# First token tile's index and DSA scores as two reduced-precision passes over the whole array, in place of float32 products on 64-row halves

## The chip, the cores and the metric

One NeuronCore of one Trainium2 chip runs the whole kernel. The metric is device microseconds of one execution. TensorE (PE in the views) does the matrix products, VectorE (DVE) and ScalarE (ACT) everything that is done by element, GpSimd (POOL) next to nothing, and SyncE (SP) issues nearly all the loads.

## The reference, cut to what matters

A decoder trunk of two layers on 256 tokens of width 1024, in float32. Each layer mixes tokens in two ways from one projection `h @ w_in`, gates and adds the two, and then runs a SwiGLU feed-forward part. The second mixer, DSA, is the one that the change touches. It scores every earlier token with a light indexer, keeps the 64 best for each query, and attends to those alone:

```python
rel = relu(einsum('bthd,bsd->bths', iq_i, ik))        # 8 index heads, 64 wide, one shared index key
score = einsum('bths,bth->bts', rel, iw_i)
score = where(key_pos <= t, score, -inf)
_, sel = lax.top_k(score, k_top)                      # 64 of the earlier tokens
s = einsum('bthd,btkhd->bhtk', q_i, gather(k, sel)) * ATTN_SCALE   # 8 heads, 64 wide
p = _masked_softmax(s, valid)
out = einsum('bhtk,btkhd->bthd', p, gather(v, sel))
```

Both score products contract over 64 numbers, half of the 128 rows of TensorE's array.

## The kernel before

The 256 tokens are two tiles of 128 (`i = 0` and `i = 1`). Weights come from memory in pieces of 1024 columns a partition (`raw`). ScalarE rounds a piece to `hi` (L164) and VectorE takes the rest as `lo` (L165). Both have the type float32r, a float32 that TensorE takes in one pass. Each dense product is three such passes (`mul3`, L173 to L175), and these 3,282 products are most of what TensorE does. The first token tile's queries see only the first 128 keys, so its score blocks are 128 x 128; the second tile's are 128 x 256.

A score product with 64 wide heads is written in one of two ways.

For the second token tile, `stack` or `twice` writes a head's rounded part and its rest into the two 64-row halves of one 128-row block, and the other operand twice, so that two float32r passes over the whole array (`score`, L335) give the product. Stacked index queries lie in `iqs`, rounded and remaining index keys in `iks`, stacked DSA keys in `dks`, doubled DSA queries in `dqs`. `iqs` and `dks` share their memory with the NSA queries `qs` (tag "qs"), `dqs` and `iks` share theirs with the NSA keys (tag "ks").

For the first token tile, plain float32 operands (`iqT`, `ikT`, `dqT`, `dkT`) are multiplied on 64 rows: even heads on rows 0 to 63, odd heads on rows 64 to 127 (L433 for the index, L661 for DSA). In the trace a float32 product shows as two records and a float32r product as one, so the 8 calls of L433 or L661 in a layer are 16 records.

Other float32 products on part of the array matter for the order: the values products of NSA and DSA (`values`, L607 and L649) use 64 of the 128 columns, and the hidden layer of NSA's compression (L517, weights `w` loaded by L515) uses 32 of them.

A scheduler decides the order of the instructions on each engine from the dependences and from its own model of time; only a few stretches are fixed by hand. Dense products of the next projection lie between the scores, the softmax steps and the values products.

Of the kernel before, what the change touches and what calls it, by code (L numbers as in the profile page):

```python
# [9 lines left out]
F32 = mybir.dt.float32  # L10
F32R = mybir.dt.float32r
AF = mybir.ActivationFunctionType
# [4 lines left out]
P = 128  # L17
SEQ = 256
NT = SEQ // P
# [12 lines left out]
HALF = (slice(0, 64), slice(64, 128))  # L32
# [47 lines left out]
def hybrid_trunk(ctx: ExitStack, tc: tile.TileContext, a: dict, out: bass.AP):  # L80
    nc = tc.nc
# [5 lines left out]
    one = ctx.enter_context(tc.tile_pool(name="one", bufs=1))  # L87
    work = ctx.enter_context(tc.tile_pool(name="work", bufs=2))
# [9 lines left out]
    def yv_bank():  # L98
        return bank("yv", 1)

    def tr_bank():
        return bank("tr", 2)

    def sc_bank():
        return bank("sc", 2)
# [209 lines left out]
    def stack(dst, src):  # L315

        for e in range(2):
            nc.scalar.activation(dst[e][HALF[e]], src[HALF[e]], AF.Copy)
        for e in range(2):
            nc.vector.tensor_sub(dst[e][HALF[1 - e]], src[HALF[e]], dst[e][HALF[e]].bitcast(F32))  # L320

    def twice(dh, dl, src):

        for e in range(2):
            nc.scalar.activation(dh[e][HALF[e]], src[HALF[e]], AF.Copy)
            nc.any.tensor_copy(dh[e][HALF[1 - e]], src[HALF[e]])
        for e in range(2):
            for h in (e, 1 - e):
                nc.vector.tensor_sub(dl[e][HALF[h]], src[HALF[e]], dh[e][HALF[e]].bitcast(F32))

    def score(o, q, k):

        pairs = [(q, t) for t in k] if isinstance(k, (list, tuple)) else [(t, k) for t in q]
        for n, (u, v) in enumerate(pairs):
            nc.tensor.matmul(o, u, v, start=n == 0, stop=n == 1)  # L335
# [3 lines left out]
    def causal(i):  # L339
        return ALL[:, P:2 * P] if i == 0 else ALL  # L340
# [12 lines left out]
    for l in range(DEPTH):  # L353
# [4 lines left out]
        ga = one.tile([P, KF * SEQ], F32, tag="bigA", name="ga")  # L358
        gb = one.tile([P, KF * SEQ], F32, tag="bigB", name="gb")

        def carve(t, o, *shape):
            n = int(np.prod(shape))
            v = t[:, o:o + n]
            return v.rearrange("p (a b) -> p a b", a=shape[0]) if len(shape) == 2 else v
# [3 lines left out]
        qT, dqT = carve(ga, 2608, 4, SEQ), carve(ga, 3632, 4, SEQ)  # L368
        accs = carve(ga, 4656, NT, SEQ)

        ks = one.tile([P, 4, NT, 2 * P], F32R, tag="ks", name="ks")
        kh, kl = [ks[:, g] for g in range(2)], [ks[:, 2 + g] for g in range(2)]
        qs = one.tile([P, 2, 4, SEQ], F32R, tag="qs", name="qs")
        ikT = carve(ga, 5168, P)
        gates = carve(gb, 0, NT, 2 * D)
        pji = carve(gb, 4096, NT, 648)
        dkT = carve(gb, 4096, 4, SEQ)
# [19 lines left out]
            load_rest(pji[:, 0, 0:1])  # L397
        iw = small.tile([P, NT, 8], F32, tag="iw", name="iw", bufs=1)
        dbias = []
        iqs = one.tile([P, 2, 4, SEQ], F32R, tag="qs", name="iqs")[:, :, :, 0:P]  # L400
        iks = one.tile([P, 4, NT, 2 * P], F32R, tag="ks", name="iks").rearrange("p a b t -> p a (b t)")[:, 0:2, 0:SEQ]
        for i in range(NT):
            nc.vector.tensor_scalar_mul(iw[:, i], pji[:, i, 576:584], 512 ** -0.5)
            rope(pji[:, i, 0:576].rearrange("p (h d) -> p h d", d=64), i, (9,))
            nc.vector.tensor_copy(pji[:, i, 576:640], pji[:, i, 512:576])
            tok = slice(i * P, (i + 1) * P)
            qp = tr_bank()
            for k in range(4):
                nc.tensor.transpose(qp[:, k * P:(k + 1) * P], pji[:, i, k * P:(k + 1) * P], ident)
            q3 = qp.rearrange("p (k t) -> p k t", t=P)  # L410
            if i == 0:
                iqT = work.tile([P, 4, P], F32, tag="pr", name="iqT", bufs=8)
                nc.scalar.activation(iqT, q3, AF.Copy)
            else:
                stack([iqs[:, e] for e in range(2)], q3)
            kp = tr_bank()[:, 0:P]
            nc.tensor.transpose(kp, pji[:, i, 512:640], ident)
            nc.scalar.activation(iks[:, 0, tok], kp, AF.Copy)
            if i == 0:
                nc.scalar.activation(ikT, kp, AF.Copy)  # L420
            nc.vector.tensor_sub(iks[:, 1, tok], kp, iks[:, 0, tok].bitcast(F32))
        for i in range(NT):
            nk = P * (i + 1)
            acc = accs[:, i, 0:nk]
            prev = causal(i)
            per = 512 // nk
            for p0 in range(0, 4, per):
                sbs = [sc_bank() for _ in range(2)]
                for p in range(p0, p0 + per):
                    outs = [sb[:, (p - p0) * nk:(p - p0 + 1) * nk] for sb in sbs]  # L430
                    if i == 0:
                        for e in range(2):
                            nc.tensor.matmul(outs[e], iqT[HALF[e], p], ikT[HALF[e]], start=True, stop=True)  # L433
                    else:
                        for e in range(2):
                            score(outs[e], iqs[:, e, p], [iks[:, z] for z in range(2)])
                for e in range(2):
                    rl = work.tile([P, 512], F32, tag="k2", name="rl", bufs=3)
                    nc.scalar.activation(rl, sbs[e], AF.Relu)
                    for p in range(p0, p0 + per):  # L440
                        h = 2 * p + e
                        nc.vector.scalar_tensor_tensor(acc, rl[:, (p - p0) * nk:(p - p0 + 1) * nk],
                                                       iw[:, i, h:h + 1], prev, ALU.mult, ALU.add)
                        prev = acc
            dbias.append(acc)
# [23 lines left out]
        for i in range(NT):  # L469
# [12 lines left out]
            kp = tr_bank()  # L482
# [3 lines left out]
            tok = slice(i * P, (i + 1) * P)  # L486
# [3 lines left out]
            q3 = qp.rearrange("p (r t) -> p r t", t=P)  # L490
# [7 lines left out]
        for kind, nm in ((0, "cmpk"), (1, "cmpv")):  # L498
# [9 lines left out]
            for half in range(2):  # L508
                q = 32 * (2 * half + kind)
                for mq in range(2):  # L510
                    r0 = half * 1024 + mq * 512
                    w1 = work.tile([P, 4, P], F32, tag="w1", name="w1", bufs=3)
# [3 lines left out]
                    for m in range(4):  # L516
                        nc.tensor.matmul(hp[q:q + 32, 0:P], blk[:, half * 8 + mq * 4 + m], w1[:, m],  # L517
                                         start=mq == 0 and m == 0, stop=mq == 1 and m == 3, tile_position=(0, q))
# [5 lines left out]
        t = small.tile([P, 2, 2, 16], F32, tag="gt", name="gt", bufs=1)  # L524
# [10 lines left out]
        kp = sc_bank()  # L535
# [102 lines left out]
        def dsa(i):  # L638
            tok = slice(i * P, (i + 1) * P)
            nk = P * (i + 1)  # L640
            per = 512 // nk
            yd = yv_bank()

            def values(p0, pts):
                for p in range(p0, p0 + per):
                    for b in range(i + 1):
                        for e in range(2):
                            v0 = (2 * p + e) * 64
                            nc.tensor.matmul(yd[e * 64:(e + 1) * 64, p * P:(p + 1) * P], dv[:, b, v0:v0 + 64],  # L649
                                             pts[e][:, (p - p0) * (i + 1) + b], start=p == 0 and b == 0,  # L650
                                             stop=p == 3 and b == i)

            done = []
            for p0 in range(0, 4, per):
                pts = []
                sbs = [sc_bank() for _ in range(2)]
                for p in range(p0, p0 + per):
                    outs = [sb[:, (p - p0) * nk:(p - p0 + 1) * nk] for sb in sbs]
                    if i == 0:
                        for e in range(2):  # L660
                            nc.tensor.matmul(outs[e], dqT[HALF[e], p, 0:P], dkT[HALF[e], p, 0:P], start=True, stop=True)  # L661
                    else:
                        for e in range(2):
                            score(outs[e], [dqs[:, z, p] for z in (e, 2 + e)], dks[:, e, p])
                for sb in sbs:
                    segs = sb.rearrange("p (h b t) -> p h b t", h=per, t=P)
                    pts.append(softmax([segs[:, h] for h in range(per)], dbias[i], None))
                done.append((p0, pts))
                if len(done) > LAG:
                    values(*done.pop(0))  # L670
            for d in done:
                values(*d)
            y_out(yd, 4, tok)
# [2 lines left out]
            nsa(i)  # L676

        dks = one.tile([P, 2, 4, SEQ], F32R, tag="qs", name="dks")
        dqs = one.tile([P, 4, NT, 2 * P], F32R, tag="ks", name="dqs").rearrange("p z b (c t) -> p z (b c) t", t=P)
        stack([dks[:, e] for e in range(2)], dkT)  # L680
        twice([dqs[:, e] for e in range(2)], [dqs[:, 2 + e] for e in range(2)], dqT[:, :, P:])
        dsa(0)
        dsa(1)


# [93 lines left out]
        for c0 in range(0, D_FF, 512):  # L779
# [12 lines left out]
            for i in range(NT):  # L792
# [3 lines left out]
                nk = n // P  # L796
# [3 lines left out]
                ks = slice(c0 // P, c0 // P + nk)  # L800
# [72 lines left out]
```

## Time and profile before

| | |
|---|---|
| median of 3 runs | 821.17 us (820.97 to 821.17) |
| the profiled execution | 821.0 us |
| its span, first to last instruction | 819.2 us |
| mean granted TensorE clock | 0.999 of full speed |
| TensorE, matrix products | 810.9 us busy, 4437 records |
| VectorE | 549.5 us busy |
| ScalarE | 461.3 us busy |
| read from memory | 138.24 MB, 170 GB/s over the span |

1.8 us of the profiled execution lie around the span. The time of one record in a list is its whole way through the array, and the next record starts long before it ends; what a record costs TensorE is the distance between starts.

### The profile page before, as it was taken

To read this page: it belongs to the slowest core of one execution; us is meant where nothing else is said; L and a number is where in the kernel's file an instruction comes from. 1 tells how busy PE (TensorE), PEld (TensorE's weight loads), DVE (VectorE), ACT (ScalarE), POOL (GpSimd) and SP (SyncE) were. 2 spreads that over 40 slices of the span, in tenths; PEclk is the share of its full clock that TensorE was granted. 3 is DMA by queue.
4 is the path that set the end of the run, shared out by engine and by line. 5 is a ranking of instruction groups with operands and counts; after the bars stand their busy time and mean duration, and the time that the engine had idled before them with its cause. 6 is when DMAs were issued, how large, how long until landed. Compare 5 with 4: busy or idle time off the path is not lost.

```text
span 819.2 us, 12201 instructions
## 1 busy us (share of the span) xinstructions
PE 810.9 (99%) x4437; PEld 679.2 (83%) x4437; DVE 549.5 (67%) x1201; ACT 461.3 (56%) x791; POOL 8.4 (1%) x18
## 2 busy tenths in 40 slices
PE   8999999999999999999999999999999999999997
PEld 7887888888888888988898888888888888889886
DVE  5799668887665555554577994889776556546445
ACT  6866358773655445444467644778556445444433
POOL 0100000000000000000000000000000000000000
PEclk9999999999999999999999999999999999999999
DMA  8955754125475664576376564542345665547651
GB/s 275 343 165 168 218 172 138 52 81 180 152 231 164 196 183 152 169 241 193 102 214 191 170 207 142 153 129 78 128 134 175 206 192 183 182 119 231 202 177 52
DMA packets 76332, 140.09 MB, mean 171 GB/s; under 512 B 5056, under 2 KB 24512, under 8 KB 76272
## 3 DMA queue, kind: packets, MB, share of 16 engines
q1 hardware_dynamic: 76032, 138.59, 54.2%
q0 software_dynamic: 240, 0.72, 0.4%
q8 instruction: 35, 0.57, 0.3%
q14 instruction: 25, 0.20, 0.1%
HBM read 138.24 MB, written 1.05 MB: 170 GB/s over the span
## 4 chain that ended last, share of the span: by engine, by line
PE 98%; DMA 1%; SPq 0%; ACT 0%; DVE 0%; issue 0%; POOLq 0%; ACTq 0%
PE mm L175 26%; PE mm L173 26%; PE mm L174 26%; PE tr L280 3%; PE sc L335 2%; PE sc L517 2%; PE yv L607 2%; PE yv L175 2%; PE yv L174 2%; PE yv L173 1%; PE tr L798 1%; PE yv L649 1%; DMA raw<-w_in 1%; PE tr L234 1%; PE yv L634 1%; PE sc L174 0%
## 5 line engine op out<-in xcount | busy, mean ns | idle before, releaser
L165 DVE TENSOR_TENSOR lo<-raw,hi 128x1024 fp32r<-128x1024 f32 (+3 forms) x264 | 301.7, 1148 | 159.2 <-ACT hi L164 155.4
L164 ACT ACTIVATE hi<-raw 128x1024 fp32r<-128x1024 f32 (+3 forms) x264 | 262.2, 1000 | 189.3 <-PE mm L175 129.0
L174 PE MATMUL mm<-lo,ah 128*128 128x512 f32 (+3 forms) x850 | 318.9, 375 | 0.0
L175 PE MATMUL mm<-hi,al 128*128 128x512 f32 (+3 forms) x850 | 318.6, 376 | 0.0
L173 PE MATMUL mm<-hi,ah 128*128 128x512 f32 (+3 forms) x850 | 317.5, 379 | 0.0
L175 PEld LDWEIGHTS mm<-hi,al 128*128 128x128 f32 x850 | 159.8, 188 | 28.4 <-issue 1.5
L174 PEld LDWEIGHTS mm<-lo,ah 128*128 128x128 f32 x850 | 160.1, 188 | 26.8 <-issue 0.3
L173 PEld LDWEIGHTS mm<-hi,ah 128*128 128x128 f32 x850 | 159.7, 188 | 27.1 <-ACT hi L164 0.3
L300 ACT ACTIVATE pr<-pr,mx 128x128 f32<-128x128 f32 (+1 forms) x96 | 42.7, 448 | 12.4 <-DVE mx L297 12.1
L174 PE MATMUL mm<-lo,hh 128*128 128x512 f32 x126 | 49.3, 391 | 0.0
L175 PE MATMUL mm<-hi,hl 128*128 128x512 f32 x126 | 49.1, 390 | 0.0
L173 PE MATMUL mm<-hi,hh 128*128 128x512 f32 x126 | 48.7, 395 | 0.0
L803 DVE TENSOR_TENSOR hl<-tr,hh 128x512 fp32r<-128x512 f32 (+1 forms) x24 | 15.5, 647 | 36.5 <-ACT hh L802 36.5
L802 ACT ACTIVATE hh<-tr 128x512 fp32r<-128x512 f32 (+1 forms) x24 | 13.5, 562 | 45.4 <-PE tr L798 45.4
L175 PEld LDWEIGHTS mm<-hi,hl 128*128 128x128 f32 x126 | 23.7, 188 | 4.9
L174 PEld LDWEIGHTS mm<-lo,hh 128*128 128x128 f32 x126 | 23.7, 188 | 4.1
L173 PEld LDWEIGHTS mm<-hi,hh 128*128 128x128 f32 x126 | 23.7, 188 | 4.2
L309 DVE TENSOR_SCALAR pr<-pr,c 128x128 f32<-128x128 f32 (+1 forms) x96 | 24.7, 316 | 0.6
L297 DVE CUSTOM_DVE_ANT_0 pr<-sc,cst 128x128 f32<-128x128 f32 (+1 forms) x64 | 19.0, 353 | 6.3 <-PE sc L335 6.0
L280 PE MATMUL tr<-cst,pr 128*128 128x128 f32 x144 | 20.7, 273 | 0.0
L789 ACT ACTIVATE sg<-mm,rstd 128x512 f32<-128x512 f32 (+1 forms) x24 | 15.7, 654 | 8.8 <-PE mm L175 8.6
L281 ACT COPY pt<-tr 128x512 f32<-128x512 f32 x32 | 17.6, 584 | 4.4 <-PE tr L280 4.4
(247 smaller groups left out, 800.3 us busy)
## 6 DMA issues: line engine op xcount, KB each, us to landing
raw<-w_in SPq DMA_DIRECT2D x72, 512.0 KB, 3.7
raw<-w_ffn_down SPq DMA_DIRECT2D x44, 512.0 KB, 4.4
raw<-w_ffn_gate SPq DMA_DIRECT2D x40, 512.0 KB, 4.5
raw<-w_ffn_up SPq DMA_DIRECT2D x40, 512.0 KB, 4.3
raw<-w_out SPq DMA_DIRECT2D x16, 512.0 KB, 4.1
raw<-w_in SPq DMA_DIRECT2D x16, 292.0 KB, 3.7
raw<-w_branch_nsa SPq DMA_DIRECT2D x16, 256.0 KB, 3.9
raw<-w_branch_dsa SPq DMA_DIRECT2D x8, 512.0 KB, 3.7
```

What stands on the lines that cost most here:

```text
L164: nc.scalar.activation(hi[:, 0:kt * n], raw[:, 0:kt * n], AF.Copy)
L165: nc.vector.tensor_sub(lo[:, 0:kt * n], raw[:, 0:kt * n], hi[:, 0:kt * n].bitcast(F32))
L173: nc.tensor.matmul(dst, xh, wh, start=first, stop=False)
L174: nc.tensor.matmul(dst, xh, wl, start=False, stop=False)
L175: nc.tensor.matmul(dst, xl, wh, start=False, stop=last)
L280: nc.tensor.transpose(tp[:, k * P:(k + 1) * P], piece, ident)
L281: nc.any.tensor_copy(dst, tp[:, 0:len(parts) * P].rearrange("p (k t) -> p k t", t=P))
L297: nc.vector.tensor_tensor_reduce(pr[:, h].rearrange("p (b t) -> p b t", t=P), v, b3, -0.125, 3.4e38, ALU.add, ALU.min, accum_out=mx[:, h:h ...
L300: nc.scalar.activation(pr[:, h], pr[:, h], AF.Exp, bias=mx[:, h:h + 1], scale=-1.0, accum_out=sm[:, h:h + 1])
L309: nc.vector.tensor_scalar_mul(pr[:, h], pr[:, h], c[:, h:h + 1])
L335: nc.tensor.matmul(o, u, v, start=n == 0, stop=n == 1)
L517: nc.tensor.matmul(hp[q:q + 32, 0:P], blk[:, half * 8 + mq * 4 + m], w1[:, m], start=mq == 0 and m == 0, stop=mq == 1 and m == 3, tile_pos ...
```

## The change

For the first token tile too, both scores are now two float32r passes over the whole array. The index queries of both tiles are stacked in `iqs`, and the copies `iqT` and `ikT` go. For DSA, the queries of the first tile are doubled and split into four new tiles `dq0` (three in the memory of tag "q2", one in that of tag "w1", which the compression weights use), and the keys come from the stacked `dks`, which the second tile used already. In a layer, 8 float32 calls for the index and 8 for DSA become 16 float32r calls each.

```diff
@@ -371,7 +371,6 @@
-        ikT = carve(ga, 5168, P)
@@ -397,7 +396,7 @@
-        iqs = one.tile([P, 2, 4, SEQ], F32R, tag="qs", name="iqs")[:, :, :, 0:P]
+        iqs = one.tile([P, 2, 4, SEQ], F32R, tag="qs", name="iqs")
@@ -408,16 +407,10 @@
-            if i == 0:
-                iqT = work.tile([P, 4, P], F32, tag="pr", name="iqT", bufs=8)
-                nc.scalar.activation(iqT, q3, AF.Copy)
-            else:
-                stack([iqs[:, e] for e in range(2)], q3)
+            stack([iqs[:, e, :, tok] for e in range(2)], q3)
             kp = tr_bank()[:, 0:P]
             nc.tensor.transpose(kp, pji[:, i, 512:640], ident)
             nc.scalar.activation(iks[:, 0, tok], kp, AF.Copy)
-            if i == 0:
-                nc.scalar.activation(ikT, kp, AF.Copy)
@@ -428,12 +421,8 @@
-                    if i == 0:
-                        for e in range(2):
-                            nc.tensor.matmul(outs[e], iqT[HALF[e], p], ikT[HALF[e]], start=True, stop=True)
-                    else:
-                        for e in range(2):
-                            score(outs[e], iqs[:, e, p], [iks[:, z] for z in range(2)])
+                    for e in range(2):
+                        score(outs[e], iqs[:, e, p, i * P:(i + 1) * P], [iks[:, z, 0:nk] for z in range(2)])
@@ -656,12 +645,8 @@
-                    if i == 0:
-                        for e in range(2):
-                            nc.tensor.matmul(outs[e], dqT[HALF[e], p, 0:P], dkT[HALF[e], p, 0:P], start=True, stop=True)
-                    else:
-                        for e in range(2):
-                            score(outs[e], [dqs[:, z, p] for z in (e, 2 + e)], dks[:, e, p])
+                    for e in range(2):
+                        score(outs[e], [dqs[i][z][:, p] for z in (e, 2 + e)], dks[:, e, p, 0:nk])
@@ -676,9 +661,12 @@
-        dqs = one.tile([P, 4, NT, 2 * P], F32R, tag="ks", name="dqs").rearrange("p z b (c t) -> p z (b c) t", t=P)
+        dq1 = one.tile([P, 4, NT, 2 * P], F32R, tag="ks", name="dqs").rearrange("p z b (c t) -> p z (b c) t", t=P)
+        dqs = [[work.tile([P, 4, P], F32R, tag=t, name="dq0", bufs=3) for t in ("q2", "q2", "q2", "w1")],
+               [dq1[:, z] for z in range(4)]]
+        twice(dqs[0][0:2], dqs[0][2:4], dqT[:, :, 0:P])
         stack([dks[:, e] for e in range(2)], dkT)
-        twice([dqs[:, e] for e in range(2)], [dqs[:, 2 + e] for e in range(2)], dqT[:, :, P:])
+        twice(dqs[1][0:2], dqs[1][2:4], dqT[:, :, P:])
```

The scheduler also puts other work in other places. Three of them, all on TensorE, follow; `sc`, `tr`, `yv` and `mm` are the accumulator banks of scores, transposes, values and dense products, and a row with `x7` stands for seven calls. Line numbers behind the change are up to 12 lower.

The first is the index in layer 0. Before, its rows are these (dense products are left out):

```order
L409 MATMUL tr<-cst,gb 128x128 x4
L433 MATMUL sc<-ga,iqT 128x128
L417 MATMUL tr<-cst,gb 128x128
L433 MATMUL sc<-ga,iqT 128x128 x7
...
L335 MATMUL sc<-iks,iqs 128x256
```

With the change they are these:

```order
L335 MATMUL sc<-iks,iqs 128x128
...
L408 MATMUL tr<-cst,gb 128x128 x4
L412 MATMUL tr<-cst,gb 128x128
L335 MATMUL sc<-iks,iqs 128x128 x15
...
L335 MATMUL sc<-iks,iqs 128x256
```

Eight calls on halves, in two stretches, have become sixteen on the whole array, also in two; in layer 1 the eight stood together.

The second place is DSA in layer 0, from the last values products of NSA's third group of heads (seven calls, L607 before, L596 now) to DSA's last values products (L649, now L638). Before:

```order
L607 MATMUL yv<-pt,ga 64x128 x7
L661 MATMUL sc<-gb,ga 128x128 x8
...
L607 MATMUL yv<-pt,ga 64x128 x8
...
L607 MATMUL yv<-pt,ga 64x128 x8
...
L649 MATMUL yv<-pt,ga 64x128 x8
...
L649 MATMUL yv<-pt,ga 64x128 x9
...
L649 MATMUL yv<-pt,ga 64x128 x7
```

With the change (names of `dq0` carry numbers; of the sixteen score calls the first and the last stand):

```order
L596 MATMUL yv<-pt,ga 64x128 x7
...
L335 MATMUL sc<-dks,dq_1580 128x128
...
L335 MATMUL sc<-dks,dq_1583 128x128
...
L596 MATMUL yv<-pt,ga 64x128
...
L596 MATMUL yv<-pt,ga 64x128 x7
...
L596 MATMUL yv<-pt,ga 64x128
...
L596 MATMUL yv<-pt,ga 64x128 x7
...
L638 MATMUL yv<-pt,ga 64x128 x8
...
L638 MATMUL yv<-pt,ga 64x128 x3
...
L638 MATMUL yv<-pt,ga 64x128 x5
...
L638 MATMUL yv<-pt,ga 64x128 x8
```

DSA's first scores no longer follow the seven values calls at once: 16 dense products stand between. The values calls behind them came in five runs (8, 8, 8, 9, 7) and come now in eight (1, 7, 1, 7, 8, 3, 5, 8). Layer 1 has both orders alike.

The third place is the compression's hidden layer in layer 0. Before, its 32 calls lie so:

```order
L517 MATMUL sc<-w_803,blk 32x128 x4
L517 MATMUL sc<-w_810,blk 32x128 x4
L517 MATMUL sc<-w_817,blk 32x128 x4
...
L517 MATMUL sc<-w_824,blk 32x128 x4
...
L517 MATMUL sc<-w_836,blk 32x128 x4
L517 MATMUL sc<-w_842,blk 32x128 x4
...
L517 MATMUL sc<-w_848,blk 32x128 x4
...
L517 MATMUL sc<-w_854,blk 32x128 x4
```

With the change:

```order
L506 MATMUL sc<-w_812,blk 32x128 x4
L506 MATMUL sc<-w_819,blk 32x128 x4
L506 MATMUL sc<-w_826,blk 32x128 x4
...
L506 MATMUL sc<-w_833,blk 32x128 x4
L506 MATMUL sc<-w_845,blk 32x128 x4
L506 MATMUL sc<-w_851,blk 32x128 x4
...
L506 MATMUL sc<-w_857,blk 32x128 x4
L506 MATMUL sc<-w_863,blk 32x128 x4
```

Five runs of 12, 4, 8, 4 and 4 calls have become three of 12, 12 and 8. In layer 1 they stay five of the same lengths.

## Rows read from the trace of the kernel before

**Rows 1.** The page: busy time of each engine, and shares of the last chain.

```profile
PE 810.9 (99%) x4437; PEld 679.2 (83%) x4437; DVE 549.5 (67%) x1201; ACT 461.3 (56%) x791; POOL 8.4 (1%) x18
...
PE 98%; DMA 1%; SPq 0%; ACT 0%; DVE 0%; issue 0%; POOLq 0%; ACTq 0%
```

**Rows 2.** Waits of TensorE: total us, times, longest.

```profile
PE tr L112 <- DVE warm L118: 1.2, 1, 1.2
```

**Rows 3.** Timeline of TensorE, index of layer 1: start us, us, records at the end.

```profile
436.43 0.49 PE L409 MATMUL tr<-cst,gb 128*128 128x128 f32 x3
436.76 0.27 PE L417 MATMUL tr<-cst,gb 128*128 128x128 f32 x1
436.96 1.16 PE L433 MATMUL sc<-ga,iqT 64*128 64x128 f32 x16
438.06 0.40 PE L173 MATMUL mm<-hi,ah 128*128 128x280 f32 x1
438.29 0.30 PE L174 MATMUL mm<-lo,ah 128*128 128x280 f32 x1
```

**Rows 4.** Timeline of TensorE, index of layer 0.

```profile
36.22 0.49 PE L433 MATMUL sc<-ga,iqT 64*128 64x128 f32 x2
36.64 0.33 PE L417 MATMUL tr<-cst,gb 128*128 128x128 f32 x1
36.90 1.16 PE L433 MATMUL sc<-ga,iqT 64*128 64x128 f32 x14
37.98 0.40 PE L173 MATMUL mm<-hi,ah 128*128 128x280 f32 x1
38.22 0.29 PE L174 MATMUL mm<-lo,ah 128*128 128x280 f32 x1
38.35 0.29 PE L175 MATMUL mm<-hi,al 128*128 128x280 f32 x1
```

**Rows 5.** Timeline of TensorE, first DSA scores of layer 0.

```profile
157.56 1.16 PE L661 MATMUL sc<-gb,ga 64*128 64x128 f32 x16
158.65 0.50 PE L173 MATMUL mm<-hi,ah 128*128 128x512 f32 x1
```

**Rows 6.** Timeline of TensorE, NSA's compressed scores (L576) and next rows, layer 0.

```profile
111.97 0.97 PE L576 MATMUL sc<-kcbd,ga 128*128 128x32 f32 x8
112.78 0.72 PE L335 MATMUL sc<-ks,qs 128*128 128x256 f32 x4
113.34 0.40 PE L175 MATMUL mm<-hi,al 128*128 128x512 f32 x1
113.57 0.40 PE L173 MATMUL mm<-hi,ah 128*128 128x512 f32 x1
```

**Rows 7.** Timeline of TensorE, values products on 64 columns, three places.

```profile
134.45 0.43 PE L607 MATMUL yv<-pt,ga 128*64 128x128 f32 x2
134.81 0.50 PE L175 MATMUL mm<-hi,al 128*128 128x512 f32 x1
135.15 0.40 PE L173 MATMUL mm<-hi,ah 128*128 128x512 f32 x1
...
178.50 1.09 PE L649 MATMUL yv<-pt,ga 128*64 128x128 f32 x16
...
184.77 1.31 PE L649 MATMUL yv<-pt,ga 128*64 128x128 f32 x18
```

**Rows 8.** Timeline of TensorE, compression products on 32 columns, three of five runs.

```profile
73.22 2.40 PE L517 MATMUL sc<-w,blk 128*32 128x128 f32 x24
...
83.08 1.94 PE L517 MATMUL sc<-w,blk 128*32 128x128 f32 x16
...
91.01 1.06 PE L517 MATMUL sc<-w,blk 128*32 128x128 f32 x8
```

**Rows 9.** Timeline of VectorE, splits of DSA keys and queries, layer 0.

```profile
155.78 2.45 DVE L320 TENSOR_TENSOR dks<-gb,dks 64x1024 fp32r<-64x1024 f32 x2
158.25 2.79 DVE L329 TENSOR_TENSOR dqs<-ga,dqs 64x512 fp32r<-64x512 f32 x4
```

## The prediction

> **What bounds the kernel now.** I read the page first, then the waits, then TensorE's timeline at the places that the change touches. The page says who is the bound: TensorE is busy 99% of the span and the chain that ended last is TensorE for 98% [rows 1]. The reader should not stop there, since records overlap in a pipeline and a busy engine need not be one at its best. The waits settle it: the longest that TensorE has is 1.2 us, and that is the start of the program [rows 2]. So nothing that VectorE, ScalarE or a transfer gains can be had back; only the starts of TensorE's own records count. The time changes by what TensorE issues more or less, and by any wait that is new. I therefore price TensorE's records by the distance between their starts.
>
> **What the halves cost now.** In layer 1 the index has 16 half-array records between two whole-array neighbours [rows 3]. The transposes ahead start 0.11 us apart (0.33 for three), so the last, at 436.76, would let the next record start at 436.87; the first half record starts at 436.96, 0.09 later. The next dense product starts at 438.06, and the one behind it 0.23 later, where two dense products of that size lie 0.13 apart in the undisturbed place [rows 4]. So 1.42 us pass from 436.87 to 438.29, of which 0.13 belong to the dense product: the halves cost 1.29 us.
>
> In layer 0 they come in two stretches with a transpose between [rows 4]. With the same 0.09 at the front the disturbance lasts from 36.13 to 38.22, 2.09 us; less the transpose (0.11) and a dense product (0.13) that is 1.85 us.
>
> For DSA they follow values products on 64 columns directly [rows 5]. That run would have to be left for the whole array in any case, so only the distance 157.56 to 158.65 goes: 1.09 us, and the same in layer 1. Together the 32 calls on halves cost 1.85 + 1.29 + 2 x 1.09 = 5.32 us.
>
> How that comes about matters for the new price. Sixteen records take 1.1 us, 0.07 each, because even and odd heads run side by side on their halves. What is lost again is the passage into and out of the mode, some 0.2 us a stretch beyond the records. Here the Trainium skill speaks against the change: "TensorEngine Tiling (Array Packing)", Performance Considerations, has products that contract over at most 64 rows share the array in two row tiles; its Tiling Modes add that a change of mode drains the engine. The trace shows both, and by the 0.07 alone the halves would cost 32 x 2 x 0.07 = 4.5 us instead of my 5.3.
>
> **What the passes cost instead.** There are 64 new float32r passes (32 a layer), each with its own stationary block of 128 columns and a stream of 128. The trace has no float32r pass with a stream under 256 columns, so I bound it. Below: a dense pass streams 512 columns in 0.23 us [rows 6], a quarter of that is 0.06. Above: if a short float32r pass ran as a float32 product does, it would be two records. What a record costs that streams little is shown by L576: eight records that stream only 32 columns each, with 128 loaded, take 0.81 us up to the next group, and with the four 256-column passes behind them 1.37 for twelve [rows 6]: 0.10 to 0.11 each. The stream would have been a quarter of the one here, so it is the load that takes 0.11. The transposes, with 128 loaded and 128 streamed, say 0.11 too [rows 3]. I take 0.111: a new pass loads as much as an L576 record, and its load cannot hide behind a stream that is shorter than itself. The upper bound is then two such records, 0.22.
>
> At 0.111 the 64 passes cost 7.10 us. Net of the halves: +1.78 us.
>
> "TensorE: Matmul & The Clock Gate" in the Trainium skill (Back-to-back issue gap) gives about 81 ns a matmul for a sustained stream of loads and 128-column products. By that the 64 passes would be 5.2 us and the whole sum 1.9 us smaller. L576's 0.11 in this trace is for the same size of load in float32, so I stay with the row.
>
> **What moves with it.** The rest of TensorE's work is the same in number, but a run of products on part of the array pays its own passage, so the number of runs counts. A single values call is two records: 134.45 to 134.81 until the next product starts, and that one needs 0.34 instead of 0.23 [rows 7]; with 0.09 at the front (as above), a run of one costs 0.56 us. Sixteen records print 1.09 us where two print 0.43, and 18 print 1.31 [rows 7]; one printed 0.43 is 0.56 in all, so a run of 8 calls costs 1.22 and of 9 calls 1.44. Calls go in pairs (two heads side by side), so a run costs 0.34 + 0.22 for each begun pair. Runs of 7 and 8 have four pairs, of 9 five, of 1 one, of 3 two, of 5 three.
>
> In DSA's stretch the five runs behind the scores (8, 8, 8, 9, 7) have 21 pairs: 5 x 0.34 + 21 x 0.22 = 6.32 us. The eight runs of the changed order (1, 7, 1, 7, 8, 3, 5, 8) have 23: 7.78 us. Two of these are followed by transposes, which lose 0.06 less at the passage than dense products do, so 7.67. That is +1.35 us a layer, +2.7 in all: a term that the edit itself doesn't name, and as large as its own.
>
> In layer 0 the compression's five runs become three. The runs of 12, 8 and 4 calls print 2.40, 1.94 and 1.06 us [rows 8], and each run pays some 0.1 around it, as the values runs do (0.56 against the printed 0.43). Before: 2.40 + 1.06 + 1.94 + 1.06 + 1.06 = 7.52 and five passages; after: 2.40 + 2.40 + 1.94 = 6.74 and three. That is -0.78 and about -0.26, together -1.04 us. In layer 1 the five runs stay, with other neighbours; I put +0.1.
>
> **What is hidden.** VectorE and ScalarE get more to do. In a layer two more splits of index queries and four of DSA queries, of the shape that takes 0.70 us [rows 9], and two copies or so make some 5 us on VectorE, against 549.5 us busy in 819 [rows 1]. They cost nothing as long as the dense products' `lo` pieces stay ahead of TensorE; if that cover goes, each us of lateness is a us of TensorE. The one new wait that I see is DSA's: its first scores need `dks` now, which can be written only when NSA's last scores have left the memory that it shares. Before, `dks` is done at 155.78 + 2.45 = 158.23 [rows 9], and VectorE's order up to there is unchanged. TensorE would come to the scores 16 dense products of 0.23 after 157.56, at 161.2. So there are 3.0 us in hand. Behind that wait stand all dense products of the gates.
>
> **Sum.** +1.78 + 2.7 - 1.04 + 0.1 = +3.5 to +3.6 us. The profiled execution took 821.0 us (819.2 of span and 1.8 around), 0.2 under the median of 821.17; both give 824.6 to 824.8. I say 824.7 us, +0.4%.
>
> **The rivals.** A measurement of this kernel tells 0.2%, 1.6 us, from no change (819.5 to 822.8 us).
>
> A, the passes stream. If the load is not the limit and a pass costs what its columns take, 0.06, the 64 passes are 3.7 us, and the whole is 3.7 - 5.32 + 1.76 = +0.1: 821.3 us, no slower than before. It decides at a price of 0.08 a pass, below which the time is within 0.2%. Against it stand L576 and the transposes, two kinds of record at 0.11. For it: neither is float32r. Chance 0.07. The 81 ns of the Trainium skill's "TensorE: Matmul & The Clock Gate" would stand just at that edge, 822.8 us.
>
> B, short passes are dear. If a float32r pass of 128 columns is worked as a float32 product, 0.22, the passes add 64 x 0.11 = 7.1 us more: 831.8 us. For it: every float32r pass in the trace has 256 columns or more. Against it: such a pass is one record wherever it stands. Chance 0.12.
>
> D, a new wait. If `dks` is more than 3 us later than it was, or VectorE's added splits delay the `lo` pieces in the stretch between the index and the hidden layer, TensorE idles. One to two us in each layer give 826 to 829 us. VectorE is two thirds busy over the span, which speaks against it; that the scheduler's own model of time set the order speaks for it. Chance 0.14.
>
> The forecast itself, a gapless TensorE with 0.111 a pass, has 0.63. What I have not seen, with a gain, gets 0.04.
>
> **Range and chances.** The forecast's own spread is small, 823.8 to 825.8: the run term rests on prices that recur, and the pass price hardly leaves 0.105 to 0.12. A lies at 821.3 to 822.8 and D reaches 829. From 821.3 to 829.0 leaves out B (0.12) and the unseen gain (0.04). Slower by over 0.2%: forecast, B and D, 0.89. Within 0.2%: A, 0.07. Faster: 0.04.
>
> **What the changed profile would show.** The 64 passes in TensorE's timeline: sixteen together should last about 1.78 us up to the next product; 1.0 would be A, 3.5 would be B. No half-array record is left, and layer 1's index loses its two passages. The values runs should stand in the eight pieces, single calls costing 0.56 each. TensorE's waits should stay at what they are; a wait of the first DSA pass for VectorE's `dks`, or of a dense pass for `lo`, is D. If the time falls although the passes cost 0.11, my prices for the runs are wrong, most of all the 2.7.

## The result, and the profile after

The changed kernel takes 826.89 us (median of 6 runs, 825.65 to 828.05), the kernel before 821.16 (6 runs, 820.77 to 821.38). The ratio is 1.0066, with an interval of 1.0055 to 1.0077: slower by 5.7 us. The forecast was 824.7 in a range of 821.3 to 829.0, so sign and range held and the middle was 2.2 us short. The profiled execution took 827.37 us (span 825.5, granted clock 0.998). Of two kernels further on, one run each came at a lower granted clock (1355.96 us at 0.556 with the index alone, its only profile, and 1007.88 us at 0.751 with a lag of zero) and is left out of the medians.

The page of the changed kernel, the two lines that answer to [rows 1]:

```profile
PE 815.7 (99%) x4437; PEld 682.1 (83%) x4437; DVE 557.5 (68%) x1212; ACT 466.1 (56%) x800; POOL 8.4 (1%) x18
...
PE 96%; DMA 1%; DVE 1%; issue 0%; ACT 0%; SPq 0%; POOLq 0%; DVEq 0%; ACTq 0%
```

The number of TensorE's records is unchanged, as 32 float32 calls were 64 records and are now 64 passes. TensorE is still 99% busy, and that is the figure that hides the story. The chain lost two points of TensorE, one of them to VectorE. Who took them stands in the waits of TensorE (total us, times, longest):

```profile
PE tr L112 <- DVE warm L118: 1.2, 1, 1.2
PE tr L710 <- DVE mg L707: 1.1, 2, 0.6
PE mm L174 <- DVE lo L165: 0.7, 3, 0.4
PE sc L174 <- DVE lo L165: 0.5, 2, 0.3
PE sc L173 <- ACT hi L164: 0.2, 1, 0.2
```

The first line and the last two are the start of the program. The kernel before had those three and no others: the line of [rows 2], and these two.

```profile
PE sc L174 <- DVE lo L165: 0.5, 2, 0.3
PE sc L173 <- ACT hi L164: 0.5, 1, 0.5
```

So the second and third lines of the changed kernel are new. Its timeline of TensorE shows them, and the new passes too (start us, us, records at the end):

```profile
38.28 1.87 PE L335 MATMUL sc<-iks,iqs 128*128 128x128 f32 x15
39.98 0.34 PE L173 MATMUL mm<-hi,ah 128*128 128x280 f32 x1
...
72.52 2.40 PE L506 MATMUL sc<-w,blk 128*32 128x128 f32 x24
...
80.11 2.40 PE L506 MATMUL sc<-w,blk 128*32 128x128 f32 x24
...
89.16 1.94 PE L506 MATMUL sc<-w,blk 128*32 128x128 f32 x16
...
160.25 1.90 PE L335 MATMUL sc<-dks,dq 128*128 128x128 f32 x16
161.98 0.45 PE L174 MATMUL mm<-lo,ah 128*128 128x512 f32 x1
162.27 0.39 PE L175 MATMUL mm<-hi,al 128*128 128x512 f32 x1
162.58 0.43 PE L596 MATMUL yv<-pt,ga 128*64 128x128 f32 x2
162.95 0.50 PE L173 MATMUL mm<-hi,ah 128*128 128x512 f32 x1
163.28 0.40 PE L174 MATMUL mm<-lo,ah 128*128 128x512 f32 x1
...
189.64 0.39 PE L175 MATMUL mm<-hi,al 128*128 128x512 f32 x1
189.96 1.09 PE L638 MATMUL yv<-pt,ga 128*64 128x128 f32 x16
191.62 0.63 PE L710 MATMUL tr<-cst,mg 128*128 128x128 f32 x4 [0.57 <-DVE mg L707]
...
618.54 0.39 PE L173 MATMUL mm<-hi,ah 128*128 128x512 f32 x1
619.30 0.50 PE L174 MATMUL mm<-lo,ah 128*128 128x512 f32 x1 [0.37 <-DVE lo L165]
619.64 0.39 PE L175 MATMUL mm<-hi,al 128*128 128x512 f32 x1
619.87 0.40 PE L173 MATMUL mm<-hi,ah 128*128 128x512 f32 x1
620.43 0.50 PE L174 MATMUL mm<-lo,ah 128*128 128x512 f32 x1 [0.17 <-DVE lo L165]
620.77 0.40 PE L175 MATMUL mm<-hi,al 128*128 128x512 f32 x1
621.01 0.39 PE L173 MATMUL mm<-hi,ah 128*128 128x512 f32 x1
621.57 0.50 PE L174 MATMUL mm<-lo,ah 128*128 128x512 f32 x1 [0.17 <-DVE lo L165]
```

Read the distances between starts. Fifteen passes take 1.70 us to the next product, sixteen take 1.73: 0.11 each. (The product behind the sixteen takes 0.29 up to the next start in place of 0.23; with these 0.06 they come to 1.79, 0.112 each.) From a single values call (162.58) to the second dense product behind it 0.70 us pass, of which 0.23 belong to the first of these products; the other 0.47, with 0.09 at the front, are the 0.56 of [rows 7]. The compression runs of layer 0 are three, at the prices of [rows 8].

The wait at L710: 16 values records take 1.02 us up to the next start (183.79 to 184.81 in a row shown further on), so the transposes could have started at 190.98; they start at 191.62, 0.64 later (the expectations below put it at 0.73). The same gap stands in layer 1, 1.28 us together. The idle time that the row prints, 0.57, is a little less, since the modelled end of a record lies behind the moment when the next could start.

The wait at `lo`, in the output product of layer 1: three distances of 0.76, 0.56 and 0.56 where 0.23 is usual, 1.19 us in all.

VectorE's timeline of the changed kernel, at both places:

```profile
190.06 0.69 DVE L706 SCALAR_TENSOR_TENSOR gb<-gb,mm 128x512 f32<-128x512 f32 x1 [2.02 <-PE mm L175]
190.78 0.69 DVE L707 TENSOR_TENSOR mg<-mg,gb 128x512 f32<-128x512 f32 x1
...
610.88 1.28 DVE L714 TENSOR_TENSOR al<-tr,ah 128x512 fp32r<-128x512 f32 x2
616.28 1.22 DVE L165 TENSOR_TENSOR spare<-raw,spare 128x1024 fp32r<-128x1024 f32 x1 [4.12 <-ACT spare L164]
617.43 0.68 DVE L714 TENSOR_TENSOR al<-tr,ah 128x512 fp32r<-128x512 f32 x1
618.03 4.62 DVE L165 TENSOR_TENSOR lo<-raw,hi 128x1024 fp32r<-128x1024 f32 x4
```

At the first place VectorE is not late or overloaded: it had been idle for 2.02 us and starts as soon as the dense product (189.64) is through. Its two operations need until 191.47, and TensorE's order has nothing but one values run of 1.02 us to lay over them. At the second place VectorE does its instructions in order: the split of the last part of `w_out` into `spare` waits 4.12 us for ScalarE and a transfer, and four `lo` pieces stand behind it. The chain that ended last has that transfer, again of the changed kernel (start us, us):

```profile
607.49 1.15 DVE lo L165
...
608.66 6.51 DMA raw<-w_out
615.19 1.07 ACT spare L164
616.28 0.52 DVE spare L165
```

The transfer starts behind a `lo` split of VectorE. From its start to the first product that reads `spare` the changed kernel would have 12.3 us without the 1.19 lost (608.66 to 622.13), and the kernel before had 12.2 (603.56 to 615.79). So it doesn't start later than it did; it takes 6.51 us, where it took 4.5 before.

### The profile page after: what moved, and what is told of

It is laid out like the page before. It is cut to its first block, busy times and chain, and to the rows that moved or that the text cites. A ratio compares the mean times of both kernels' runs of the same rounds, so it can differ in the third digit from the quotient of the medians.

```text
span 825.5 us, 12238 instructions
## 1 busy us (share of the span) xinstructions
PE 815.7 (99%) x4437; PEld 682.1 (83%) x4437; DVE 557.5 (68%) x1212; ACT 466.1 (56%) x800; POOL 8.4 (1%) x18
## 4 chain that ended last, share of the span: by engine, by line
PE 96%; DMA 1%; DVE 1%; issue 0%; ACT 0%; SPq 0%; POOLq 0%; DVEq 0%; ACTq 0%
PE mm L173 25%; PE mm L175 25%; PE mm L174 25%; PE sc L335 3%; PE tr L280 3%; PE yv L596 2%; PE sc L506 2%; PE yv L174 1%; PE yv L175 1%; PE yv L173 1%; PE tr L786 1%; DMA raw<-w_out 1%; DMA raw<-w_in 1%; PE tr L234 1%; PE yv L638 1%; DVE lo L165 1%
```

## The experiments

Two theories went in, with a rival on the price. Theory 1: the passes cost 0.111 us, the runs what the forecast says, and the rest is waits that come with TensorE's new order around DSA. Rival 2: VectorE's added splits delay TensorE, wherever they stand. Rival 3: a pass costs 0.153 us, which would explain all that is left over. The kernel before took 821.07 to 821.17 us (medians) beside these runs.

**Index alone.** Index scores by passes, DSA scores by halves as before:

```diff
-                        score(outs[e], [dqs[i][z][:, p] for z in (e, 2 + e)], dks[:, e, p, 0:nk])
+                        if i == 0:
+                            nc.tensor.matmul(outs[e], dqT[HALF[e], p, 0:P], dkT[HALF[e], p, 0:P], start=True, stop=True)
+                        else:
+                            score(outs[e], [dqs[:, z, p] for z in (e, 2 + e)], dks[:, e, p])
```

> Index scores of the first tile by passes, DSA scores on halves as before, so that TensorE's order around DSA is that of before. Theory 1 (prices and order): 32 passes at 0.111 us (+3.55) for halves of 3.14, three compression runs in place of five in layer 0 (-1.04), +0.1 in layer 1: -0.5 us, 820.6 to 820.7 us, and neither the wait of the merged gate's transposes (0.73 us in each layer of the changed kernel) nor the waits for lo behind the output product. Rival 2 (the added VectorE work delays TensorE wherever it stands): a third of the added splits are here, so a third of the 2.7 us of new waits: 821.5 us. Rival 3 (a pass costs more than its spacing, 0.153 us, the rest of the time after): 822.0 us.

Measured: 820.77 us, ratio 0.9999 (0.999 to 1.0008). Theory 1's 820.7 fits; rival 3's 822.0 lies above the interval (821.8 at its upper end), rival 2's 821.5 within it. Whether the two waits are absent is not shown.

**DSA alone.** The other half of the change, index on halves (the edit is the diff of the change without its index hunks).

> DSA scores of the first tile by passes, index scores on halves as before. Theory 1: 32 passes (+3.55) for halves of 2.18, and in TensorE's order now nine and eight values runs behind the scores in place of five, +4.3 us in all, and the merged gate's transposes again right behind the last values run: 0.73 us in each layer. Together 827.0 us, 825.5 if that wait is not there: all that the change loses, and more, comes from DSA's part. Rival 2: two thirds of the waits, 827.3 us, but as waits for lo. Rival 3: 826.8 us without any wait.

Measured: 826.98 us, ratio 1.0071 (1.0058 to 1.0083). All of the loss is DSA's. The three totals expected (826.8 to 827.3) all lie in the interval, so it is the waits of TensorE that tell them apart. Apart from the start of the program they have the transposes' wait alone, and none for `lo`, against rival 2:

```profile
PE tr L721 <- DVE mg L718: 1.1, 2, 0.6
```

**Keys of their own.** The changed kernel, all 64 passes kept, with the first tile's keys also in memory of their own. That adds two splits a layer to VectorE, and frees the first DSA scores from waiting for NSA's last:

```diff
+        dk0 = [work.tile([P, 4, P], F32R, tag="w1", name="dk0", bufs=3) for _ in range(2)]
+        stack(dk0, dkT[:, :, 0:P])
...
-                        score(outs[e], [dqs[i][z][:, p] for z in (e, 2 + e)], dks[:, e, p, 0:nk])
+                        score(outs[e], [dqs[i][z][:, p] for z in (e, 2 + e)],
+                              dk0[e][:, p] if i == 0 else dks[:, e, p])
```

> The changed kernel, with the first tile's stacked DSA keys also in memory of their own, so that its DSA scores need not wait for NSA's to leave the shared memory (two more splits on VectorE, all 64 passes kept). In TensorE's order six values runs stand where the change had eight, and dense products stand between the last values run and the merged gate's transposes. Theory 1 (the loss beyond the passes is the order's): values runs +0.56 us a layer instead of +1.35, no wait of these transposes: +1.8 us against before, 823.0 us; with the waits for lo still there 824.2. Rival 2 (VectorE's added work): more of it than in the changed kernel, so 826 us or more. Rival 3 (a pass costs 0.153): 825.7 us.

Measured: 822.86 us, ratio 1.0021 (1.0012 to 1.003). Four of the 5.7 us are gone although VectorE does more and every pass is still there. Rivals 2 and 3 fall. The waits of this kernel have neither `mg` nor `mm ... lo`; all that is left is the start of the program.

**Passes twice.** Every short pass issued a second time:

```diff
-                        score(outs[e], iqs[:, e, p, i * P:(i + 1) * P], [iks[:, z, 0:nk] for z in range(2)])
+                        for _ in range(2 - i):
+                            score(outs[e], iqs[:, e, p, i * P:(i + 1) * P], [iks[:, z, 0:nk] for z in range(2)])
```

and the same at DSA's `score`.

> The changed kernel, each short pass of the index and DSA scores of the first tile issued twice (128 passes in place of 64, the second pair overwriting the first). Theory 1: 64 x 0.111 = +7.1 us against the changed kernel, 834.0 us, and a spacing of 0.11 us throughout. If passes streamed at 0.06 where they stand in longer rows: +3.8, 830.7 us. Rival 3 (0.153): +9.8, 836.7 us.

Measured: 834.05 us, ratio 1.0155 (1.0142 to 1.0169), 7.2 us above the changed kernel. That total by itself is weaker than it looks, because the waits of TensorE moved once more: the transposes' is gone, one for `ah` has come in both layers, and the one for `lo` now stands in layer 0.

```profile
PE mm L173 <- ACT ah L557: 1.4, 2, 0.7
...
PE mm L174 <- DVE lo L165: 0.8, 3, 0.4
```

They sum to 2.2 us, against 1.8 of `mg` and `lo` in the changed kernel, so it is by chance that they nearly cancel. The price of a pass rests on the spacing: TensorE's timeline has 31 passes in 3.49 us, 0.113 each:

```profile
38.19 3.66 PE L335 MATMUL sc<-iks,iqs 128*128 128x128 f32 x31
41.68 0.34 PE L173 MATMUL mm<-hi,ah 128*128 128x280 f32 x1
```

**The changed kernel with the values loops exchanged.** In the scheduler's order a values run begins as soon as its first call is ready, and that is the call of the head whose probabilities come first; the other head's come later, and a run splits into 1 and 7. With the later head first, a run can't begin before both are there:

```diff
-                            for g in range(2):
+                            for g in (1, 0):
                                 nc.tensor.matmul(yn[g * 64:(g + 1) * 64, r * P:(r + 1) * P],
...
-                        for e in range(2):
+                        for e in (1, 0):
                             v0 = (2 * p + e) * 64
```

> The changed kernel with nothing but the two heads (or groups) of the innermost values loops issued in the other order, the one whose probabilities are ready last first. In TensorE's order all values runs become runs of eight calls, nine a layer (14 before, 14 plus splits in the changed kernel), and dense products stand between the last values run and the merged gate's transposes. All 64 passes are kept. Theory 1 (the runs and the wait are the loss, at 0.34 us a run and 0.22 a pair): runs and passes together 48.1 us against 49.7 of before, so 819.5 us, faster than before and some 7 us under the changed kernel. If the number of runs cost nothing (the 2.7 us mis-sized, another cause for the loss): 823 us with the wait gone, or 826 or more.

Measured: 819.64 us, ratio 0.9981 (0.9972 to 0.999). (A layer had 11 values runs before and 14 in the changed kernel; the expectation speaks of 14 before, which is wrong.) All passes are in it, and it is 7.3 us under the changed kernel and faster than the kernel before. In its timeline the last two values runs have dense products behind them, and between the last of them and the merged gate's transposes stand 35 dense products, without idle time:

```profile
183.79 1.09 PE L638 MATMUL yv<-pt,ga 128*64 128x128 f32 x16
184.81 0.50 PE L173 MATMUL mm<-hi,ah 128*128 128x512 f32 x1
...
185.71 1.09 PE L638 MATMUL yv<-pt,ga 128*64 128x128 f32 x16
186.73 0.50 PE L173 MATMUL mm<-hi,ah 128*128 128x512 f32 x1
...
194.82 0.60 PE L710 MATMUL tr<-cst,mg 128*128 128x128 f32 x4
```

**The kernel before with the same exchange.**

> The kernel before with the same exchange in the values loops, halves kept. Nine values runs a layer in place of eleven: Theory 1 -2.6 us, 818.6 us, so that passes against halves on equal runs come to +0.9 us (819.5 against 818.6). If runs cost nothing: 821.1 us.

Measured: 819.46 us, ratio 0.9979 (0.997 to 0.9987), 0.9 short of the gain. Part of it is a wait that the new order brought, in TensorE's and ScalarE's timelines of this kernel:

```profile
174.96 1.04 PE L280 MATMUL tr<-cst,pr 128*128 128x128 f32 x8
176.08 0.51 PE L173 MATMUL mm<-hi,ah 128*128 128x512 f32 x1
```

```profile
175.46 0.57 ACT L567 CAST ah<-yv 128x512 fp32r<-128x512 f32 x1
```

Eight transposes at 0.11 end at 175.84, and the product starts at 176.08, because its `ah` is written from 175.46 on. That is 0.24 us, and the same in layer 1. The remaining 0.4 us stay open.

**Token tile first.** The changed kernel, with the loops over the second branch's products exchanged, so that other dense products stand between the last gate product and the transposes:

```diff
-        for j in range(2):
-            w = branch_weights(1, j)
-            for i in range(NT):
-                branch(1, j, i, w)
+        w = [branch_weights(1, j) for j in range(2)]
+        for i in range(NT):
+            for j in range(2):
+                branch(1, j, i, w[j])
```

> The changed kernel with the second branch's products issued by token tile first, then by column half. In TensorE's order six dense products and more now stand ahead of the merged gate's first transposes, and the last values run of eight is split into one and seven. Theory 1: the two waits of 0.73 us are gone, the two splits cost 0.62 each: -0.2 us against the changed kernel, 826.6 us if the waits for lo stay, 825.4 if they go as well. If the wait for mg were no loss of its own (it only moves to another instruction): +1.2 us, 828.1 us.

Measured: 826.4 us, ratio 1.0064 (1.0051 to 1.0076). Inconclusive in its total, since the last values run was split in exchange. Its waits of TensorE have no `mg` and no `mm ... lo` any more. At equal places its trace tells more: it is 0.37 us behind the changed kernel's at the first DSA pass (160.62 against 160.25), from the start of the program on, and 0.46 behind at a product of layer 1 (458.77 against 458.31). So in layer 0 the wait of 0.64 went and the split of 0.62 came, which is about even, as expected.

**Index passes in layer 0 alone, values loops exchanged.** On the kernel before, with `l == 0` as the condition for the index passes:

```diff
-                    if i == 0:
+                    if i == 0 and l:
                         for e in range(2):
                             nc.tensor.matmul(outs[e], iqT[HALF[e], p], ikT[HALF[e]], start=True, stop=True)
```

> The kernel before with the exchanged values loops, and with index scores by passes in the first layer alone, where the halves cost 1.85 us, 16 passes 1.78 and the compression runs go from five to three. Theory 1: 46.1 us of runs and passes against 49.7, so 817.5 us, the best of all here, 1.1 under the kernel before with the exchange alone. If the passes' place does not matter: 818.6 us.

Measured: 817.91 us, ratio 0.9961 (0.9949 to 0.9974), the best kernel of this study, 3.2 us under the kernel before. It is 0.4 above the 817.5 of theory 1 and 1.55 under the exchange alone (819.46), where 1.1 was expected; none of its runs (817.6 to 818.23) reaches one of that kernel's (818.85 to 819.65). So in layer 0 the index passes, with the fewer compression runs that come with them, are a gain.

**The changed kernel again.**

> The changed kernel once more, unaltered, for a second profile. The merged gate's wait is in the program's order, so two gaps of 0.84 us between the last values run and these transposes must stand in it again. The three gaps of 0.55 to 0.75 us in front of products with lo in the second layer's output product hung, in the first profile, on one transfer of 6.5 us: if that is chance, they are absent this time, the last part of w_out lands in some 4.5 us, and the time of the profiled run is 1.2 us lower, 826.2 us. If the order brings them, they stand there again.

Measured: 827.0 us, ratio 1.0073 (1.0061 to 1.0085); the profiled run 826.56. The waits of TensorE, and the transfer in the chain:

```profile
PE tr L710 <- DVE mg L707: 1.1, 2, 0.6
...
PE mm L174 <- DVE lo L165: 0.2, 1, 0.2
```

```profile
608.66 5.68 DMA raw<-w_out
```

The transposes' wait is the same. The other one is neither absent nor the same: two gaps of 0.40 and 0.57 (0.51 us too much) behind a transfer of 5.68 us, where 6.51 us had made 1.19. So the order leaves little in hand there, and the length of the transfer goes with how much is lost. The same part of `w_out` landed after 4.5 us in the kernel before, 4.7 with DSA alone, 4.8 with the token tile first and 5.3 with keys of their own, all without this wait; after 5.7 it cost 0.51 us, after 6.5 it cost 1.19.

**The best kernel with a lag of zero.** One constant, which in this kernel brings DSA's last values run and the transposes together again, with halves in DSA and none of its added splits:

```diff
-LAG = 1
+LAG = 0
```

> The best kernel so far (exchanged values loops, index passes in the first layer alone), with the values of a group issued at once (a lag of zero in place of one). DSA's scores of the first tile stay on halves. The number and size of the runs stay, but in TensorE's order the merged gate's transposes stand right behind DSA's last values run again, as in the changed kernel. If that place costs 0.73 us a layer whatever else the kernel does: 819.2 us (817.9 + 1.47 - 0.16). If the wait comes from the passes or from VectorE's added splits: 817.8 us.

Measured: 818.62 us, ratio 0.997 (0.9959 to 0.9981). Both totals expected (819.2 and 817.8) lie in the interval, so it is the timeline of TensorE that decides. It has the gap:

```profile
186.66 1.09 PE L651 MATMUL yv<-pt,ga 128*64 128x128 f32 x16
188.32 0.52 PE L724 MATMUL tr<-cst,mg 128*128 128x128 f32 x3 [0.57 <-DVE mg L721]
```

188.32 - 186.66 - 1.02 is 0.64 us again. So the wait belongs to the place and not to the passes or to the splits that they add. The total rose by 0.7 and not by 1.3 us: in the lag-one kernel a product had waited for `ah` as in the kernel before with the exchange, some 0.25 us a layer (174.51 - 173.41 is 1.10, where eight transposes took 0.84 in the kernel before), and here none does.

## Why the forecast was right, and where it was short

**Passes at 0.111 us: right.** 0.113 and 0.108 in the timeline of the changed kernel (0.112 with the passage behind them), and 0.113 in the kernel with twice as many. Its 7.2 us for 64 more, where 7.1 were expected, agree too, though with other waits in them. Rivals A and B fall with it.

**Values and compression runs: right in the main.** A single call cost 0.56, and the eight pieces stand as forecast. With as many records behind it (2,159), layer 1 begins 1.58 us later than before (405.10 against 403.52). The forecast's terms for layer 0 (-0.07 and +0.69 for index and DSA, +1.35, -1.04), with the 0.64 of the transposes' wait, sum to 1.57. For layer 1 both waits and the forecast's terms make 4.5, and 4.7 were measured. That shows the sums and not each term: on the kernel before, the exchange of the loops gave 0.4 us less than the run prices said, beyond its new wait. Restoring the runs took the loss away, and the waits with it, with all passes in place (822.86 and 819.64). On runs of equal number, passes and halves differ by 0.2 us (819.64 against 819.46), within what these runs can tell; 0.9 was expected, and the halves' side carries the two waits of 0.24 for `ah`. So the edit by itself is close to neutral, and most of what it costs is the order that it causes. Shown by the own-keys kernel: the order comes from the first tile's scores having to wait until NSA's last scores leave the memory that the stacked keys share.

**`dks` with 3 us in hand: right.** Its splits end at 157.19 (154.72 + 2.47 in VectorE's timeline), and the first DSA pass at 160.25 waited for nothing.

**A gapless TensorE: the step that failed.** The forecast was +3.5; the transposes' wait adds 1.28 and the wait for `lo` 1.19, together 6.0, and 821.0 + 6.0 = 827.0 against 827.37 profiled. For the second profile, 3.5 + 1.28 + 0.51 makes 826.3 against 826.56. The 826.89 lie outside the forecast's own spread (823.8 to 825.8): what came is nearer to rival D, with a chance of 0.14, than to the forecast with its 0.63, and the stated range held because D had been taken into it. D had the size (826 to 829) and the kind, but not the place or the cause: I looked for it at `dks` and at `lo` ahead of the hidden layer, from VectorE's added splits. It sat behind the last values run, and there the working had already been: I wrote that "two of these are followed by transposes, which lose 0.06 less at the passage", and took the gain of 0.06 without asking what the transposes read. From the start of the last dense product (189.64) over VectorE's two operations to the transposes (191.62) it takes 1.98 us, and TensorE has 0.32 to the values run and 1.02 in it: 0.64 us a layer uncovered. The order was known and the two operations stood in the trace of before, so this could have been worked out beforehand.

**`lo` stays ahead: wrong in one place.** The wait hung on one long transfer and on VectorE's order, with `spare` ahead of four `lo` pieces. It came in both profiles of the changed kernel and, in layer 0, in that of the passes-twice kernel, but not in the DSA-alone, own-keys and token-tile-first kernels. In the passes-twice kernel that transfer took 6.6 us as well. What made it slow was not found.

## What to carry to other kernels

On a bound TensorE that runs products on part of its array, count the runs before the products: here the exchange of two loop indices was worth 1.7 us in the kernel before and, with the waits that it also removed, 7.3 in the changed one, more than the 5.7 of the edit under study. And when a change moves instructions, go through the new neighbours pair by pair: for each, ask what the second one reads, how long the engine that writes it needs, and whether what stands in between is as long.

## What was not expected of the hardware

A float32r pass of 128 columns with a load of 128 starts every 0.108 to 0.113 us, twice what its columns alone would take by a dense pass (0.23 for 512, so 0.06 for 128) and the same as a float32 transpose (0.11). "TensorE: Matmul & The Clock Gate" of the Trainium skill (Back-to-back issue gap) has about 81 ns for a stream of loads and products of that size; no row here shows so little for these passes. And transfers of one size differ: of the last three parts of `w_out` (512 KB each) in layer 1 of the first profile of the changed kernel the median landed in 4.3 us, the last in 6.5 (5.7 in the second profile), enough to use up VectorE's lead.
